# A separate tile for the third pair of quarter sums in a two-layer decoder trunk

## The chip, the cores and the metric

The kernel runs on one NeuronCore of a Trainium2 chip. The metric is the device time of one execution in microseconds (us); lower is better. Where a spread is given, it is that of three timed executions.

## The reference

A trunk of two layers over 256 tokens of width 2048, all in fp32. Layer 0 mixes tokens with forgetting attention (16 heads of 128), layer 1 with a mixture of three dilated windows (8 heads). Each mixer and each MLP stands behind an RMSNorm and adds into the residual stream:

```
def sq_relu_mlp(h, w_up, w_down):
    a = jax.nn.relu(h @ w_up)          # (256 x 2048) @ (2048 x 8192)
    return (a * a) @ w_down            # (256 x 8192) @ (8192 x 2048)

for i in range(DEPTH):                 # DEPTH = 2
    h = rms_norm(x, mix_norm_g[i])
    x = x + (fox_attention if i % 2 == 0 else dilated_attention)(h, ...)
    h = rms_norm(x, mlp_norm_g[i])
    x = x + sq_relu_mlp(h, mlp_w_up[i], mlp_w_down[i])
```

The change concerns the two MLPs, above all their product with `w_up`.

## The kernel before

**Tiles and engines.** Every weight matrix is read once from HBM, in tiles of 256 rows by 512 columns (512 KB, here called a *raw*: two row blocks of 128 x 512). TensorE (PE) multiplies in fp32r, so each raw is split into a high part and a low part: ScalarE (ACT) copies the raw into `wh` (L403), VectorE (DVE) subtracts that from the raw into `wl` (L404). A product is three matmuls, high x high, high x low, low x high, of 512 columns each (L452 to L454 for a plain raw, L1108 to L1110 for what follows).

**Units.** The raws are loaded in the order of a list `plan`, and split and multiplied in the order of a list `units`. There are `W_BUFS` = 5 pairs of `wh` and `wl`: when PE has used a unit, `split` prepares the unit five places later. There are `RAW_BUFS` = 5 raw buffers. After each split `next_load` marks in `spent` the raws that are no longer needed, moves the counter `done` forward over them, *in the order of the plan*, and issues loads until five raws beyond `done` are under way. All those loads (L378) stand in one queue, SyncE's (SP), which issues in order and waits at each load until the buffer it writes is free. The same queue carries the round trips through memory that transpose the activations: four writes `held` and one read `back` for each tile (L359).

**Wide halves.** Five of the 16 column groups of each `w_up` (list `WIDE`) are computed in pairs of column groups by seven products of half-size blocks in place of eight (the Strassen-Winograd scheme). For each pair of row blocks `pr` = 0 to 7, two raws are loaded crosswise: X1 holds the quarters B11 and B22, X2 holds B12 and B21. From them come three pairs of half-size operands, each a unit of its own and each with two products (`PRODUCTS`), so six matmuls:

- *crossed*: DVE first makes the differences X2 - B22 in a tile `quarters` with the tag `sd` (L400). Then X2 itself is split. Then DVE makes the third pair, one sum and one difference of quarters, **in place in X2** (L406, L407).
- *differences*: the tile `quarters` is split.
- *sums*: the third pair is split, read from X2's buffer.

A fourth kind (`what` = 3) is one plain product for each row pair. These units are woven in between plain raws of the other products, so that the order of units round a slot is: crossed, differences, a plain raw R0, sums, one or two more plain raws, the next crossed. In the plan the order is X1, X2, R0, R1, (R2), next X1, next X2. `add_slot` and `wide_slots` lay this down when the program is written; nothing is decided at run time.

**What the raw buffers do round a slot.** After the split of *crossed* X1 is spent and X2 is not, so `done` stops at X2: one load is issued there. After *differences* and R0 none is. After *sums* X2 and R0 are spent together, and two loads are issued.

**Token sums.** The other operand of those products are sums of blocks of the normalized activations. `token_sums` makes them for each `pr`, in a tile `room`, and splits them into a high and a low tile. These 16 tiles have to live through the whole MLP and lie in buffers that the attention layers use: the list `SUM_TAGS` names them, `vh` and `vl` (the attention values' two parts) for `pr` = 6, `pT` and `t1` for `pr` = 7. The tag `s` with five buffers holds the scores and is idle during the MLP but for the tables of the second mixer.

**After a wide half** `wide_chain` combines the six PSUM banks, squares, and hands over to `turn_up`, which transposes the result by the round trip `turned`, `held`, `back` and splits it into `aTh` and `aTl` (L1051, L1055, L1058), the operands of the product with `w_down`.

Of the kernel before, what the change touches and what calls it, by code (L numbers as in the profile page):

```python
# [9 lines left out]
F32 = mybir.dt.float32  # L10
F32R = mybir.dt.float32r
# [6 lines left out]
P = 128  # L18
# [3 lines left out]
NC = 512  # L22
NX = D // NC
KC = D // P
# [13 lines left out]
RAW_SUB = 2  # L38
PARTS = ((0, 12), (12, 16))
OUT_PARTS = ((0, 12), (12, 14), (14, 16))  # L40
S_BUFS = 5
# [2 lines left out]


PRODUCTS = (((0, 1, 5), (1, 0, 0)), ((2, 0, 1), (3, 1, 3)), ((4, 0, 2), (5, 1, 6)))
SUM_TAGS = ("kh3", "kl3", "kh4", "kl4", "kh5", "kl5", "q0", "q1", "q2", "qkw0", "qkw1", "qkw2", "vh", "vl", "pT", "t1")

WIDE = ((1, 0), (2, 0), (2, 2), (3, 0), (3, 2))
WIDE_FROM = 15  # L50
# [74 lines left out]
def trunk(ctx: ExitStack, tc, x, fox_w_in, fox_b_f, fox_q_gain, fox_k_gain, fox_w_out, dil_w_in,  # L125
          dil_q_gain, dil_k_gain, dil_w_out, mix_norm_g, mlp_norm_g, mlp_w_up, mlp_w_down, out):
    nc = tc.nc
# [5 lines left out]
    def clear(steps):  # L133

        return steps + (jobs.now + steps + 1 + shift[0]) % 2
# [21 lines left out]
    work = ctx.enter_context(tc.tile_pool(name="work", bufs=1))  # L157
# [210 lines left out]
    raws, splits = [], []  # L368

    def load():  # L370
        i = state["raw"]
        if i >= len(plan):
            return
        t = wpool.tile([P, RAW_SUB, NC], F32, tag="raw", name=f"raw{i}", bufs=RAW_BUFS)
        for (k, columns), src in plan[i]:
            hold(t)
            for rows in [slice(x, x + 1) for x in range(RAW_SUB)] if i == 1 else [None]:
                nc.sync.dma_start(t[:, k if rows is None else rows, columns], src if rows is None else src[:, rows])  # L378
        raws.append(t)
        state["raw"] += 1  # L380

    def split(parts=(slice(0, W_SUB),)):
        i = state["split"]
        if i >= len(units):
            return
        hi = wpool.tile([P, W_SUB, NC], F32R, tag="wh", name=f"wh{i}", bufs=W_BUFS)
        lo = wpool.tile([P, W_SUB, NC], F32R, tag="wl", name=f"wl{i}", bufs=W_BUFS)
        splits.append((hi, lo))
        state["split"] += 1
        for part in parts:  # L390
            split_part(i, part)
        if parts:
            next_load()

    def split_part(i, part):
        n, of = units[i]
        raw, (hi, lo) = raws[n], splits[i]
        if of == "crossed":
            sums_of[0] = work.tile([P, RAW_SUB, NC], F32, tag="sd", name=f"quarters{n}", bufs=1)
            nc.vector.tensor_sub(sums_of[0], raw, raws[n - 1][:, 1, :].unsqueeze(1).to_broadcast([P, RAW_SUB, NC]))  # L400
        elif of == "differences":
            raw = sums_of[0]
        nc.scalar.copy(hi[:, part, :], raw[:, part, :])  # L403
        nc.vector.tensor_sub(lo[:, part, :], raw[:, part, :], hi[:, part, :].bitcast(F32))  # L404
        if of == "crossed":
            nc.vector.tensor_add(raw[:, 0, :], raw[:, 0, :], sums_of[0][:, 1, :])  # L406
            nc.vector.tensor_sub(raw[:, 1, :], raws[n - 1][:, 0, :], raw[:, 0, :])  # L407

    sums_of, spent = [None], set()

    def next_load():


        n, of = units[state["split"] - 1]
        spent.update({"rows": (n,), "crossed": (n - 1,), "sums": (n,)}.get(of, ()))
        while state["done"] in spent:
            state["done"] += 1
        while state["raw"] < min(len(plan), state["done"] + RAW_BUFS):
            load()
# [3 lines left out]
    def in_turn(w, apart=NC // 2):  # L423
        return w.rearrange("p (b h n) -> p b n h", n=apart, h=2)
# [135 lines left out]
    def token_sums(tag):  # L560


        to = work.tile([P, 4, P], F32, tag="vw", name=f"room_{tag}", bufs=1)
        for pr in range(KC // 2):
            yield (tag, pr)
            yield clear(4)
            whole = hT[tag][pr]
            nc.vector.tensor_add(to.rearrange("p (i t) n -> p i (t n)", i=2), whole[:, :, 0, :].bitcast(F32),
                                 whole[:, :, 1, :].bitcast(F32))
            a12, a22, a11, a21 = (to[:, i, :] for i in range(4))  # L570
            nc.vector.tensor_add(a21, a21, a22)
            nc.vector.tensor_sub(a11, a11, a21)
            nc.vector.tensor_add(to[:, 0:2, :], to[:, 0:2, :], a11.unsqueeze(1).to_broadcast([P, 2, P]))
            yield 2
            hi, lo = (work.tile([P, 4, P], F32R, tag=SUM_TAGS[2 * pr + x], name=f"sums_{tag}_{pr}_{x}", bufs=1)
                      for x in range(2))
            nc.scalar.copy(hi, to)
            yield 1
            nc.vector.tensor_sub(lo, to, hi.bitcast(F32))
            sumT[tag, pr] = hi, lo  # L580
            jobs.done.add(("sums", tag, pr))

    sumT = {}
# [171 lines left out]

    def values(name):
        whole = work.tile([P, NC], F32, tag="vw", name=f"{name}w", bufs=1)
        v_hi, v_lo = (work.tile([P, NC], F32R, tag=f"v{x}", name=f"{name}{x}", bufs=1) for x in "hl")
        return whole, v_hi, v_lo

    def scores(ps, t, q, k, i):

# [335 lines left out]
    def slot_steps(tag, banks, what, pr, then):  # L1098

        hi, lo = splits[used[0]]  # L1100
        for bank, i, a, of in [(0, i, 4, pr + i) for i in range(2)] if what == 3 else [(*x, pr) for x in PRODUCTS[what]]:
            wh, wl = (in_turn(w[:, i, :]) for w in (hi, lo))
            if a < 4:
                ah, al = (x[:, a, :] for x in sumT[tag, of])
            else:
                ah, al = (hT[tag][of][:, a % 2, x, (a - 4) // 2 * P:((a - 4) // 2 + 1) * P] for x in range(2))
            alone = {"skip_group_check": bank == 0}
            nc.tensor.matmul(banks[bank], ah, wh, start=what < 3 and of == 0, stop=False, **alone)  # L1108
            nc.tensor.matmul(banks[bank], ah, wl, start=False, stop=False, **alone)
            nc.tensor.matmul(banks[bank], al, wh, start=False, stop=of == KC // 2 - 1, **alone)  # L1110
        then()
        used[0] += 1
        split()
        shift[0] ^= 1
        jobs.tick()

    def mlp(tag, **after):
# [3 lines left out]
        def one(b, n, what, pr):  # L1121
            if pr == 0 and what in (0, 2):
                pools = ((ps_acc, f"acc{1 - turn['only']}"),) if what else ((ps_tp, "tp"), (ps_sc, "sc"))
                banks[2 * what:] = [pool.tile([P, NC], F32, tag=of, name=f"wide_{tag}_{b}_{n}_{of}{i}")
                                    for pool, of in pools for i in range(2)]
            if what < 3:
                jobs.need(("sums", tag, pr))

            def then():
                if what == 2 and pr == KC // 2 - 1:  # L1130
                    jobs.spawn(wide_chain(list(banks), tag, b, n, aTs[b]))
                if what == 3 and pr == KC // 2 - 2:
                    jobs.reach((f"{tag}a{b}", "crossed", n))

            slot_steps(tag, banks, what, pr, then)

        jobs.spawn(token_sums(tag))
        woven.update(count=0, do=one, due={})
        for at, slot in wide_slots():
# [58 lines left out]
    row_blocks = [slice(i, i + 1) for i in range(W_SUB)]  # L1198
    split(())
    split_part(0, row_blocks[0])  # L1200
    jobs.spawn(first(0))
    split_part(0, row_blocks[1])
    next_load()
    split(())
    split_part(1, row_blocks[0])
# [4 lines left out]
    def opening():  # L1210
        yield 1
        split_part(1, row_blocks[1])
        next_load()
        yield 2
        split(row_blocks)
        yield 1
        split()
        for _ in range(5):
            yield 2
            split()  # L1220
        yield 1
        del issued["opening"]
        while state["split"] - used[0] < W_BUFS:
            yield 4
            split()
# [7 lines left out]
    tag = "n0"  # L1233
    for j in range(4):
        qT, kT = zip(*(heads_pairs(f"f{j}_{i}", i) for i in range(2)))
        vt = values(f"fv{j}")
        product(keys_h(tag), lhs_h(tag), lambda acc: qk_chain(
            acc, tag, ("fq", j), [(0, 2, FOX_G, qT[0]), (2 * P, 2, FOX_G, qT[1])]))
        if j == 0:
            jobs.need("wf")  # L1240
            gate(tag)
        product(keys_h(tag), lhs_h(tag), lambda acc: qk_chain(
            acc, tag, ("fk", j), [(0, 2, FOX_G + 1, kT[0]), (2 * P, 2, FOX_G + 1, kT[1])]))

        for hh in range(4):
            jobs.spawn(fox_head(j, hh, qT, kT, vt))
        product(keys_h(tag), lhs_h(tag), lambda acc: v_chain(acc, tag, ("fv", j), vt))
# [42 lines left out]
```

## Time and profile before

| | |
|---|---|
| median of three runs | 2124.59 us (2123.57 to 2125.57) |
| the profiled execution's own time | 2127.25 us |
| its span, first to last instruction | 2125.5 us |
| PE busy | 2091.7 us (98%) |
| DVE busy | 1733.9 us (82%) |
| ACT busy | 1288.6 us (61%) |
| moved by DMA | 539.02 MB, mean 254 GB/s |
| wide halves of the first MLP | from 402.1 us to 928 us of the span |
| wide halves of the second MLP | from 1500.4 us to 2023 us of the span |

Busy time counts an engine as busy while at least one of its instructions is under way. Matmuls overlap, and a PE that is fed without a pause is busy all the time; a row of waits names the instruction that waited, then the one that ended the wait, and gives the total in us, the number of times, and the longest. PEld is TensorE's loading of the stationary operand, which waits a little before the matmul does.

### The profile page before, as it was taken

To read this page: it belongs to the slowest core of one execution; us is meant where nothing else is said; L and a number is where in the kernel's file an instruction comes from. 1 tells how busy PE (TensorE), PEld (TensorE's weight loads), DVE (VectorE), ACT (ScalarE), POOL (GpSimd) and SP (SyncE) were. 2 spreads that over 40 slices of the span, in tenths; PEclk is the share of its full clock that TensorE was granted. 3 is DMA by queue.
4 is the path that set the end of the run, shared out by engine and by line. 5 is a ranking of instruction groups with operands and counts; after the bars stand their busy time and mean duration, and the time that the engine had idled before them with its cause. 6 is when DMAs were issued, how large, how long until landed. Compare 5 with 4: busy or idle time off the path is not lost.

```text
span 2125.5 us, 28747 instructions
## 1 busy us (share of the span) xinstructions
PE 2091.7 (98%) x9835; PEld 1819.3 (86%) x9835; DVE 1733.9 (82%) x2213; ACT 1288.6 (61%) x1775; POOL 135.0 (6%) x142
## 2 busy tenths in 40 slices
PE   9999999989999999999999999999999999999999
PEld 7888888878888888888888888888787888888888
DVE  6888876998889889887768787767998899898874
ACT  6565654756566657574656565646666576666562
POOL 2000000000010011010001010000000100110100
PEclk9999999999999999999999999999999999999999
DMA  8889887778898898897977776868778888988895
GB/s 255 254 263 271 249 248 232 242 229 256 252 282 270 253 280 262 266 283 247 283 236 238 245 237 210 269 205 242 243 230 274 263 276 264 272 268 272 264 290 169
DMA packets 385875, 539.02 MB, mean 254 GB/s; under 512 B 43753, under 2 KB 177217, under 8 KB 385729
## 3 DMA queue, kind: packets, MB, share of 16 engines
q1 hardware_dynamic: 371488, 524.21, 78.4%
q0 software_dynamic: 13824, 12.59, 3.7%
q8 instruction: 77, 1.26, 0.2%
q14 instruction: 70, 0.57, 0.1%
q10 hardware_dynamic: 416, 0.39, 0.1%
HBM read 484.09 MB, written 40.39 MB: 247 GB/s over the span
## 4 chain that ended last, share of the span: by engine, by line
PE 53%; DVE 21%; DMA 15%; issue 5%; ACT 3%; SPq 2%; DVEq 0%; ACTq 0%
PE acc L454 15%; PE acc L452 15%; PE acc L453 15%; DVE wl L404 11%; DMA raw<-in_mlp_w_up_dram 10%; DVE quarters L400 3%; DMA raw<-in_mlp_w_down_dram 2%; ACT wh L403 2%; DVE raw L406 2%; SPq L359 1%; DMA back_n1a<-held_n1a 1%; DMA back_n3a<-held_n3a 1%; DMA held_n1a<-turned_n1a 1%; DVE turned_n3a L1026 1%; DVE turned_n1a L1026 1%
## 5 line engine op out<-in xcount | busy, mean ns | idle before, releaser
L403 ACT CAST wh<-raw 128x1024 fp32r<-128x1024 f32 (+1 forms) x843 | 867.1, 1044 | 652.8 <-PE acc L454 283.6
L404 DVE TENSOR_TENSOR wl<-raw,wh 128x1024 fp32r<-128x1024 f32 (+1 forms) x843 | 1007.0, 1213 | 276.3 <-ACT wh L403 267.2
L452 PE MATMUL acc<-wh,hT_n 128*128 128x512 f32 x1280 | 488.0, 381 | 0.0
L453 PE MATMUL acc<-wl,hT_n 128*128 128x512 f32 x1280 | 486.9, 380 | 0.3 <-DVE wl L404 0.3
L454 PE MATMUL acc<-wh,hT_n 128*128 128x512 f32 x1280 | 486.3, 380 | 0.0
L453 PEld LDWEIGHTS acc<-wl,hT_n 128*128 128x128 f32 x1280 | 242.9, 190 | 35.3 <-DVE wl L404 2.5
L454 PEld LDWEIGHTS acc<-wh,hT_n 128*128 128x128 f32 x1280 | 242.6, 190 | 34.7 <-DVE hT_n L600 0.4
L452 PEld LDWEIGHTS acc<-wh,hT_n 128*128 128x128 f32 x1280 | 242.8, 190 | 34.0 <-ACT a_n1a L1003 0.4
L454 PE MATMUL acc<-wh,aTl_n1a 128*128 128x512 f32 x512 | 195.5, 382 | 4.6 <-DVE aTl_n1a L1058 2.3
L452 PE MATMUL acc<-wh,aTh_n1a 128*128 128x512 f32 x512 | 195.3, 381 | 2.5 <-ACT y_n L963 2.5
L453 PE MATMUL acc<-wl,aTh_n1a 128*128 128x512 f32 x512 | 195.3, 381 | 0.0
L454 PE MATMUL acc<-wh,aTl_n3a 128*128 128x512 f32 x480 | 182.3, 380 | 2.8 <-DVE aTl_n3a L1058 2.3
L452 PE MATMUL acc<-wh,aTh_n3a 128*128 128x512 f32 x480 | 182.5, 380 | 0.8 <-ACT y_n L963 0.7
L453 PE MATMUL acc<-wl,aTh_n3a 128*128 128x512 f32 x480 | 182.2, 380 | 0.9 <-DVE wl L404 0.9
L400 DVE TENSOR_TENSOR quarters<-raw,raw 128x1024 f32<-128x1024 f32 x80 | 97.8, 1222 | 67.3 <-DMA raw<-in_mlp_w_up_dram 56.6
L964 POOL DMA_DIRECT2D x<-y_n x96 | 84.4, 1360 | 995.4 <-ACT y_n L963 789.1
L403 ACT CAST wh<-quarters 128x1024 fp32r<-128x1024 f32 x80 | 83.8, 1047 | 51.8 <-DVE quarters L400 49.9
L454 PEld LDWEIGHTS acc<-wh,aTl_n1a 128*128 128x128 f32 x512 | 97.3, 190 | 20.0 <-DVE aTl_n1a L1058 3.1
L452 PEld LDWEIGHTS acc<-wh,aTh_n1a 128*128 128x128 f32 x512 | 97.2, 190 | 17.5 <-ACT y_n L963 3.7
L453 PEld LDWEIGHTS acc<-wl,aTh_n1a 128*128 128x128 f32 x512 | 97.2, 190 | 14.6 <-DVE wl L404 0.8
L454 PEld LDWEIGHTS acc<-wh,aTl_n3a 128*128 128x128 f32 x480 | 90.7, 189 | 17.0 <-DVE aTl_n3a L1058 3.1
L452 PEld LDWEIGHTS acc<-wh,aTh_n3a 128*128 128x128 f32 x480 | 90.7, 189 | 15.4 <-ACT y_n L963 2.4
(673 smaller groups left out, 2902.8 us busy)
## 6 DMA issues: line engine op xcount, KB each, us to landing
raw<-in_mlp_w_up_dram SPq DMA_DIRECT2D x296, 512.0 KB, 4.8
raw<-in_mlp_w_down_dram SPq DMA_DIRECT2D x256, 512.0 KB, 5.7
raw<-in_dil_w_in_dram SPq DMA_DIRECT2D x192, 256.0 KB, 3.7
raw<-in_fox_w_in_dram SPq DMA_DIRECT2D x94, 512.0 KB, 4.8
raw<-in_fox_w_out_dram SPq DMA_DIRECT2D x32, 512.0 KB, 5.0
raw<-in_dil_w_in_dram SPq DMA_DIRECT2D x32, 512.0 KB, 5.9
raw<-in_dil_w_out_dram SPq DMA_DIRECT2D x32, 512.0 KB, 4.4
x<-y_n POOLq DMA_DIRECT2D x96, 128.0 KB, 7.3
```

Source lines behind the costliest of these rows:

```text
L359: nc.sync.dma_start(dst, src)
L400: nc.vector.tensor_sub(sums_of[0], raw, raws[n - 1][:, 1, :].unsqueeze(1).to_broadcast([P, RAW_SUB, NC]))
L403: nc.scalar.copy(hi[:, part, :], raw[:, part, :])
L404: nc.vector.tensor_sub(lo[:, part, :], raw[:, part, :], hi[:, part, :].bitcast(F32))
L406: nc.vector.tensor_add(raw[:, 0, :], raw[:, 0, :], sums_of[0][:, 1, :])
L452: nc.tensor.matmul(acc[t], ah[:, tok], hi, start=first, stop=False)
L453: nc.tensor.matmul(acc[t], ah[:, tok], lo, start=False, stop=False)
L454: nc.tensor.matmul(acc[t], al[:, tok], hi, start=False, stop=last)
L964: nc.gpsimd.dma_start(xt[n][:, t, h * HC:h * HC + HC], y, accum_op=ALU.add)
L1026: nc.vector.transpose(tiles[t].rearrange("p (j b r) -> p b j r", j=4, b=4), rows[t].rearrange("p (b j c) -> p b j c", j=4, c=32))
```

## The change

1. The third pair of quarters no longer overwrites X2. It is written into a tile of its own with the tag `v`, one buffer of 128 x 2 x 512, made in *crossed* beside the tile `sd`; *sums* is split from it.
2. `next_load` therefore counts both X1 and X2 as spent after *crossed*, and none after *sums*.
3. The tag `v` is what `vh` and `vl` were: the attention values' two parts become one tile with two halves.
4. The token sums of `pr` = 6 take `pT` and `t1`. Those of `pr` = 7 go into three tiles of the tag `s`, each 128 x 3 x 128: three of the four blocks' high parts in the first, their low parts in the second, the fourth block's two parts in the third. Their split takes two copies and two subtractions in place of one each.

```
-SUM_TAGS = (..., "qkw2", "vh", "vl", "pT", "t1")
+SUM_TAGS = (..., "qkw2", "pT", "t1")
...
         if of == "crossed":
-            sums_of[0] = work.tile([P, RAW_SUB, NC], F32, tag="sd", name=f"quarters{n}", bufs=1)
-            nc.vector.tensor_sub(sums_of[0], raw, raws[n - 1][:, 1, :].unsqueeze(1).to_broadcast([P, RAW_SUB, NC]))
-        elif of == "differences":
-            raw = sums_of[0]
+            quarters[:] = [work.tile([P, RAW_SUB, NC], F32, tag=x, name=f"{x}_{n}", bufs=1) for x in ("sd", "v")]
+            nc.vector.tensor_sub(quarters[0], raw, raws[n - 1][:, 1, :].unsqueeze(1).to_broadcast([P, RAW_SUB, NC]))
+        elif of != "rows":
+            raw = quarters[("differences", "sums").index(of)]
         nc.scalar.copy(hi[:, part, :], raw[:, part, :])
         nc.vector.tensor_sub(lo[:, part, :], raw[:, part, :], hi[:, part, :].bitcast(F32))
         if of == "crossed":
-            nc.vector.tensor_add(raw[:, 0, :], raw[:, 0, :], sums_of[0][:, 1, :])
-            nc.vector.tensor_sub(raw[:, 1, :], raws[n - 1][:, 0, :], raw[:, 0, :])
+            nc.vector.tensor_add(quarters[1][:, 0, :], raw[:, 0, :], quarters[0][:, 1, :])
+            nc.vector.tensor_sub(quarters[1][:, 1, :], raws[n - 1][:, 0, :], quarters[1][:, 0, :])
...
-        spent.update({"rows": (n,), "crossed": (n - 1,), "sums": (n,)}.get(of, ()))
+        spent.update({"rows": (n,), "crossed": (n - 1, n)}.get(of, ()))
...
+            if pr < KC // 2 - 1:
+                split_sums = [[work.tile([P, 4, P], F32R, tag=SUM_TAGS[2 * pr + x], ...) for x in range(2)]]
+            else:
+                three = [work.tile([P, 3, P], F32R, tag="s", name=f"sums_{tag}_{pr}_{x}", bufs=S_BUFS) for x in range(3)]
+                split_sums = [three[0:2], (three[2][:, 0:1, :], three[2][:, 1:2, :])]
...
     def values(name):
         whole = work.tile([P, NC], F32, tag="vw", name=f"{name}w", bufs=1)
-        v_hi, v_lo = (work.tile([P, NC], F32R, tag=f"v{x}", name=f"{name}{x}", bufs=1) for x in "hl")
-        return whole, v_hi, v_lo
+        both = work.tile([P, 2, NC], F32R, tag="v", name=f"{name}hl", bufs=1)
+        return whole, both[:, 0], both[:, 1]
```

More of the change, by code (lines that the diff above doesn't have):

```diff
@@ L46 @@
 PRODUCTS = (((0, 1, 5), (1, 0, 0)), ((2, 0, 1), (3, 1, 3)), ((4, 0, 2), (5, 1, 6)))
-SUM_TAGS = ("kh3", "kl3", "kh4", "kl4", "kh5", "kl5", "q0", "q1", "q2", "qkw0", "qkw1", "qkw2", "vh", "vl", "pT", "t1")
+SUM_TAGS = ("kh3", "kl3", "kh4", "kl4", "kh5", "kl5", "q0", "q1", "q2", "qkw0", "qkw1", "qkw2", "pT", "t1")
 WIDE = ((1, 0), (2, 0), (2, 2), (3, 0), (3, 2))
@@ L405, in split_part @@
         if of == "crossed":
-            nc.vector.tensor_add(raw[:, 0, :], raw[:, 0, :], sums_of[0][:, 1, :])
-            nc.vector.tensor_sub(raw[:, 1, :], raws[n - 1][:, 0, :], raw[:, 0, :])
-    sums_of, spent = [None], set()
+            nc.vector.tensor_add(quarters[1][:, 0, :], raw[:, 0, :], quarters[0][:, 1, :])
+            nc.vector.tensor_sub(quarters[1][:, 1, :], raws[n - 1][:, 0, :], quarters[1][:, 0, :])
+    quarters, spent = [], set()
     def next_load():
         n, of = units[state["split"] - 1]
-        spent.update({"rows": (n,), "crossed": (n - 1,), "sums": (n,)}.get(of, ()))
+        spent.update({"rows": (n,), "crossed": (n - 1, n)}.get(of, ()))
         while state["done"] in spent:
@@ L574, in token_sums @@
             yield 2
-            hi, lo = (work.tile([P, 4, P], F32R, tag=SUM_TAGS[2 * pr + x], name=f"sums_{tag}_{pr}_{x}", bufs=1)
-                      for x in range(2))
-            nc.scalar.copy(hi, to)
+            if pr < KC // 2 - 1:
+                split_sums = [[work.tile([P, 4, P], F32R, tag=SUM_TAGS[2 * pr + x], name=f"sums_{tag}_{pr}_{x}", bufs=1)
+                               for x in range(2)]]
+            else:
+                three = [work.tile([P, 3, P], F32R, tag="s", name=f"sums_{tag}_{pr}_{x}", bufs=S_BUFS) for x in range(3)]
+                split_sums = [three[0:2], (three[2][:, 0:1, :], three[2][:, 1:2, :])]
+            sumT[tag, pr] = tuple([x[:, i, :] for x, _ in parts for i in range(x.shape[1])] for parts in
+                                  (split_sums, [pieces[::-1] for pieces in split_sums]))
+            at = 0
+            spans = []
+            for hi, lo in split_sums:
+                spans.append(to[:, at:at + hi.shape[1], :])
+                nc.scalar.copy(hi, spans[-1])
+                at += hi.shape[1]
             yield 1
-            nc.vector.tensor_sub(lo, to, hi.bitcast(F32))
-            sumT[tag, pr] = hi, lo
+            for (hi, lo), of in zip(split_sums, spans):
+                nc.vector.tensor_sub(lo, of, hi.bitcast(F32))
             jobs.done.add(("sums", tag, pr))
@@ L1103, in slot_steps @@
             if a < 4:
-                ah, al = (x[:, a, :] for x in sumT[tag, of])
+                ah, al = (x[a] for x in sumT[tag, of])
             else:
```

## The prediction

> **What bounds the kernel now.** I read the page first, then the waits of TensorE's weight loads (PEld), then the waits of VectorE (DVE), each for the whole span and for the stretches of the wide halves.
>
> ```profile
> span 2125.5 us, 28747 instructions
> PE 2091.7 (98%) x9835; PEld 1819.3 (86%) x9835; DVE 1733.9 (82%) x2213; ACT 1288.6 (61%) x1775; POOL 135.0 (6%) x142
> ```
>
> PE is busy for 98% of the span, and the change removes no matmul. All it can give back is idle time, 2125.5 - 2091.7 = 33.8 us. The largest item of that idle time is this, as the weight loads see it, and behind it stands a wait of DVE's:
>
> ```profile
> PEld wide_n_sc L1109 <- DVE wl L404: 19.6, 17, 3.7
> DVE quarters L400 <- DMA raw<-in_mlp_w_up_dram: 56.6, 36, 2.9
> ```
>
> The bank `wide_n_sc` belongs to the unit *differences*. Seventeen times PE stood there because the low part of the differences wasn't ready; and 36 times DVE, before it could even begin a slot (L400), stood idle for a raw. A slot's chain on DVE is long: L400, the low part of crossed, L406, L407, the low part of differences. When the raw is late, that last step is late. The same wait by stretches, in this order: 400 to 470, 470 to 500, 500 to 940, 1490 to 1565, 1565 to 1600, 1600 to 2030 us:
>
> ```profile
> PEld wide_n_sc L1109 <- DVE wl L404: 6.7, 3, 3.3
> PEld wide_n_sc L1109 <- DVE wl L404: 0.5, 1, 0.5
> PEld wide_n_sc L1109 <- DVE wl L404: 3.1, 4, 1.3
> PEld wide_n_sc L1109 <- DVE wl L404: 6.1, 3, 3.7
> PEld wide_n_sc L1109 <- DVE wl L404: 0.4, 2, 0.2
> PEld wide_n_sc L1109 <- DVE wl L404: 2.8, 4, 1.4
> ```
>
> Nearly two thirds lie in the first wide half of each MLP. That stage differs from the others:
>
> ```profile
> 426.00:463.00 37.00, 31.62 (x136) 25.96 (x134) 34.06 (x44) 19.64 (x26) 0.00 (x0) 0.95 0.70 223
> 1526.00:1561.00 35.00, 30.14 (x129) 24.36 (x127) 32.53 (x43) 19.88 (x26) 0.00 (x0) 0.95 0.71 232
> 570.00:640.00 70.00, 70.00 (x326) 61.31 (x325) 63.44 (x66) 47.66 (x60) 7.04 (x8) 1.00 0.89 277
> 740.00:830.00 90.00, 86.64 (x398) 74.33 (x397) 77.91 (x78) 58.68 (x72) 10.57 (x12) 1.00 0.90 275
> ```
>
> The columns are the stretch's length, busy PE, PEld, DVE, ACT, POOL, then granted clock, DMA share and GB/s. In the first two rows DVE is busy for 34.06 of 37 us and 32.53 of 35 us, because the token sums are made there too: DVE sets the pace, and DMA runs at 0.70. In the last two DVE has more room and DMA is at 0.90.
>
> **Why the raw is late.** One slot, seen on SP's queue and on DVE:
>
> ```profile
> 773.85 2.64 SPq L378 DMA_DIRECT2D raw<-in_mlp_w_up_dram  x2
> 773.13 0.69 DVE L407 TENSOR_TENSOR raw<-raw,raw 128x512 f32<-128x512 f32 x1
> 773.74 1.22 DVE L404 TENSOR_TENSOR wl<-quarters,wh 128x1024 fp32r<-128x1024 f32 x1
> 774.88 2.36 DVE L404 TENSOR_TENSOR wl<-raw,wh 128x1024 fp32r<-128x1024 f32 x2
> 782.68 1.22 DVE L400 TENSOR_TENSOR quarters<-raw,raw 128x1024 f32<-128x1024 f32 x1 [2.88 <-DMA raw<-in_mlp_w_up_dram]
> ```
>
> The first load (next X1) goes out at 773.85, when L407 ends. The second (next X2) goes out about 2.64 - 0.37 = 2.3 us later (an issue takes some 0.4 us), behind the low part of R0: it stands in the queue at the split of *sums*, where X2 is released in the program before. The X2 that it brings is what DVE waits 2.88 us for.
>
> **The change, part by part.** *The loads.* With the third pair in a tile of its own, both loads stand at *crossed* and wait for L407 alone; the next one waits for R0's low part instead of that of *sums*. In the slot shown X2 is issued at some 774.2 instead of 776.1, 1.9 us earlier. Where the queue carried a round trip in between, more is won. Next come three such places in the first wide halves, one by SP and DVE:
>
> ```profile
> 420.13 0.39 SPq L378 DMA_DIRECT2D raw<-in_mlp_w_up_dram  x1
> 425.88 0.98 SPq L378 DMA_DIRECT2D raw<-in_mlp_w_up_dram  x2
> 446.23 4.95 SPq L378 DMA_DIRECT2D raw<-in_mlp_w_up_dram  x2
> 1517.70 0.39 SPq L378 DMA_DIRECT2D raw<-in_mlp_w_up_dram  x1
> 1524.38 0.98 SPq L378 DMA_DIRECT2D raw<-in_mlp_w_up_dram  x2
> 426.25 2.35 DVE L404 TENSOR_TENSOR wl<-raw,wh 128x1024 fp32r<-128x1024 f32 x2
> 429.98 1.23 DVE L400 TENSOR_TENSOR quarters<-raw,raw 128x1024 f32<-128x1024 f32 x1 [1.37 <-DMA raw<-in_mlp_w_up_dram]
> ```
>
> X2 would go out some 5.3, 4.2 and 6.3 us earlier there (the difference less one issue). Where three plain raws lie between two slots this holds; where two lie between, X2's load stands at the earlier *crossed* already and only a plain raw comes sooner. DVE's idle time for raws is, from 400 to 470, 1490 to 1565, 500 to 940 and 1600 to 2030 us:
>
> ```profile
> DVE quarters L400 <- DMA raw<-in_mlp_w_up_dram: 2.4, 2, 1.4
> DVE quarters L400 <- DMA raw<-in_mlp_w_up_dram: 1.9, 1, 1.9
> DVE quarters L400 <- DMA raw<-in_mlp_w_up_dram: 22.6, 13, 2.9
> DVE quarters L400 <- DMA raw<-in_mlp_w_up_dram: 24.6, 16, 2.8
> ```
>
> *First wide halves.* DVE works without a pause here but for these waits, so PE gets back only what DVE gets back: 2.4 us and 1.9 us. The lead of 4.2 us and more covers waits of at most 1.9 us, so I take all of it, and the rest of the 6.7 and 6.1 us stays, as DVE's own work. The small waits from 470 to 500 (0.5) and 1565 to 1600 (0.4 in two) follow waits for a raw and go: 0.4 + 0.1, by the rate of the next paragraph. Together 2.4 + 0.4 + 1.9 + 0.1 = 4.8 us.
>
> *The other wide halves.* What an idle weight load costs PE:
>
> ```profile
> 864.22 0.38 PE L1108 MATMUL wide_n_sc<-wh,sums_n 128*128 128x512 f32 x1
> 865.20 0.19 PEld L1109 LDWEIGHTS wide_n_sc<-wl,sums_n 128*128 128x128 f32 x1 [1.01 <-DVE wl L404]
> 865.52 0.38 PE L1110 MATMUL wide_n_sc<-wh,sums_n 128*128 128x512 f32 x1
> ```
>
> Fed without a pause a matmul takes 70.00 / 326 = 0.215 us (the stretch 570 to 640). Here two took 865.52 - 864.22 = 1.30 us, 0.87 too much for an idle of 1.01: 0.14 less than the row says. The eight waits (3.1 in 4, 2.8 in 4, longest 1.4) cost 5.9 - 8 x 0.14 = 4.8 us. The longest is 1.4 us and the least lead some 1.9 us, so all eight go, even though DVE's waits of up to 2.9 us shrink to about 1 and don't vanish: the five units prepared ahead cover that. One of them (810 us) stands at a slot whose own X2 isn't earlier; it goes only because DVE comes out of the slot before it sooner. The bounds of this part are 0 and 4.8.
>
> *DVE's arithmetic.* L400, L406 and L407 keep their sizes; only the output of the last two moves. Nothing waits for the tile `v`: the previous *sums* was split earlier on the same engine. Cost 0. If that order failed, DVE would wait for one low part, 1.22 us (the L404 row above), 80 times; the program's order excludes it.
>
> *Token sums of the last pair.* One subtraction more and one copy more for each MLP. The operation that is cut in two:
>
> ```profile
> 413.29 0.68 DVE L579 TENSOR_TENSOR sums_n<-room_n,sums_n 128x512 fp32r<-128x512 f32 x1
> ```
>
> The two parts do the same work; the second adds between nothing and a whole 0.68 us, 1.4 us for both MLPs if nothing hid it, and less by far since it is a quarter of the size. I take 0 and leave the rest to the range; the cover is DVE's slack after the fifth slot. *Tags.* `t1` is taken one pair sooner, long after the squares of the norm that use it were issued; the `s` tiles are freed before the second mixer's tables need them; the values' two parts are written one behind the other and read together. I count these at 0. If a tag were still held, ACT's copy of the sums would wait, and behind it all high parts.
>
> **The sum.** 4.8 + 4.8 = 9.6 us. The profiled execution took 2127.25 us, 1.75 more than its span; it would take 2117.65. It lies 2.66 above the median of the three runs, so for the median I forecast 2124.59 - 9.6 = 2115.0 us, with a range of its own of 2112 to 2119.
>
> **The rivals.** *DMA is full, and X2 lands no sooner.* In the later halves DMA's share is 0.89 to 0.90, so loads issued sooner may only queue longer. Then the eight waits there stay, and the first halves, at 0.70, still give 4.8: 2119.8 us. Against it: between 773.85 and 776.1 SP had issued one raw and held the next back. By the row's share a tenth of DMA's time is free. [...]
>
> *Round trips come late: slower.* The reads `back` and the writes `held` that stand between *crossed* and *sums* now stand behind two more loads in SP's queue and in the DMA engines. ACT runs in order, so a cast L1051 that waits for `back` holds up every high part behind it, and with them PE.
>
> ```profile
> DMA to landing us min/median/max: 3.7/5.7/8.6
> L1051 ACT CAST aTh_n1a<-back_n1a x26: 610/614/624, 431.0 to 925.7; 128x512 fp32r<-128x512 f32 x26
> L1051 ACT CAST aTh_n3a<-back_n3a x26: 610/614/619, 1529.8 to 2020.7; 128x512 fp32r<-128x512 f32 x26
>   DMA back_n1a<-held_n1a: 0.6, 1
> ```
>
> The first line is for the reads `back`, the last is ACT's idle time for them within the first MLP's wide halves. The program allows six steps of six matmuls, 36 x 0.215 = 7.7 us, from the read to the cast; the median landing leaves 2.0 us. Two raws more ahead are 1.05 MB, at 275 GB/s 3.8 us. So a pair could be 1.8 us late; with 26 pairs in the two MLPs and about 1 us of it reaching PE behind the units prepared ahead, that is 26 us, less the 9.6: 2141 us. It decides from 0.4 us a pair. Against it: only 0.6 us of such waits today, the bytes are the same, and those moves stood behind loads that waited for the same DVE work already.
>
> *The clock too: faster still.*
>
> ```profile
> 434.80:438.20 3.40, 0.88 (x4) 0.80 (x5) 3.37 (x6) 2.64 (x4) 0.00 (x0) 1.00 0.65 204
> 438.20:441.60 3.40, 3.40 (x10) 2.50 (x9) 3.40 (x4) 1.86 (x3) 0.00 (x0) 0.50 0.43 100
> ```
>
> After a stretch in which PE was busy for 0.88 of 3.4 us the granted clock was 0.50 for 3.4 us. The mean clock of 0.95 over 37 and 35 us in the two first halves (above) says that it happened once in each, and cost 1.85 and 1.75 us. With those waits shortened by 1.4 and 1.9 us the halving may not come: some 3.4 us more, 2111.6. I don't count it, since DVE sets the pace there, and what PE gains it waits out at the next slot. [...]
>
> *The change does not do what it says.* If the buffer that X2's load takes is one freed only at *sums*, nothing moves: 2124.6 us. For it: the second load goes out at the end of R0's low part, not that of *sums*, so the buffers aren't handed out in the plan's order. Against it: at *crossed* two are free at once.
>
> **How the numbers follow.** Forecast 0.52, full DMA 0.14, late round trips 0.12, clock 0.11, no move 0.11. A measurement here can tell 0.2%, 4.2 us: faster means below 2120.3. The forecast and the clock are faster, full DMA lies at the edge and I give it 0.08 and 0.06: faster 0.71, same 0.17, slower 0.12. The range runs from the clock case with 2 us of spare, 2109.5, to no move, 2124.6, and leaves out the slow case.
>
> **What would show it.** Two loads L378 at the end of each L407; SP's wait for `sums` gone. DVE's 56.6 us for raws at L400 down to a third or less. PEld's 19.6 us at `wide_n_sc` down to about 8, all of it in the first halves. Wrong if ACT waits for `back` by several us, if the eight later waits are still there, or if PE's idle time falls at L1109 and grows elsewhere.

## The result, and the profile after

| | before | after |
|---|---|---|
| median | 2124.69 us (2123.57 to 2125.57, four runs) | 2096.99 us (2096.43 to 2100.19, four runs) |
| ratio | | 0.9873 (95% interval 0.9856 to 0.9890) |
| the profiled execution and its span | 2127.25, 2125.5 us | 2096.45, 2094.6 us |

The change takes 27.7 us off, nearly three times the 9.6 us of the forecast, and the time lies below the range. The sign was right, the size was not. The chances were set on "faster" by 0.71.

These lines of the page answer to those of before: the span, the busy times, and the chain of work that ended last, by engine.

```profile
span 2094.6 us, 28771 instructions
PE 2080.3 (99%) x9835; PEld 1825.0 (87%) x9835; DVE 1730.1 (83%) x2215; ACT 1294.0 (62%) x1777; POOL 134.8 (6%) x142
PE 87%; DVE 6%; DMA 3%; issue 1%; ACT 1%; SPq 1%; POOL 0%; DVEq 0%; ACTq 0%; POOLq 0%
```

Before, the last of these read:

```profile
PE 53%; DVE 21%; DMA 15%; issue 5%; ACT 3%; SPq 2%; DVEq 0%; ACTq 0%
```

The chain that sets the end used to run through PE for half of its length, and through DVE and the DMA for over a third. Now it is PE for 87%. Two things in the first two lines deserve a look. PE's *busy* time fell by 11.4 us although it does the same 9835 matmuls. And the span of the profiled execution fell by 2125.5 - 2094.6 = 30.9 us, nearly all of the 33.8 us that the prediction held to be the most there was.

The slot that the prediction showed looks like this now (the timeline of the changed kernel, a slot of the same wide half; columns are start, duration, engine, line):

```profile
767.64 1.22 DVE L400 TENSOR_TENSOR sd<-raw,raw 128x1024 f32<-128x1024 f32 x1
769.91 0.69 DVE L406 TENSOR_TENSOR v<-raw,sd 128x512 f32<-128x512 f32 x1
770.63 0.69 DVE L407 TENSOR_TENSOR v<-raw,v 128x512 f32<-128x512 f32 x1
770.66 1.06 SPq L378 DMA_DIRECT2D raw<-in_mlp_w_up_dram  x2
```

Two loads go out nearly together: the first at 770.66, when L406 ends, the second some 0.7 us later, when L407 ends. L400 has no wait before it. The waits of the whole span, in the order of the prediction's list (the weight loads, then DVE, then SP's queue for the first and for the second of these loads):

```profile
PEld wide_n_sc L1120 <- DVE wl L404: 9.7, 5, 2.9
DVE sd L400 <- DMA raw<-in_mlp_w_up_dram: 8.1, 13, 2.5
SPq L378 <- DVE v L406: 142.9, 68, 3.1
SPq L378 <- DVE v L407: 17.6, 67, 1.6
```

Before they were 19.6 us in 17, 56.6 us in 36, and this:

```profile
SPq L378 <- DVE raw L407: 271.7, 70, 6.2
```

That row is the wait of the one load that stood at *crossed* then, so it answers to the 142.9 us of L406; the 17.6 us are all that the second load waits beyond it.

**Where the other 20 us came from.** The quickest reading is to count matmuls in stretches of equal length. Before, then after, from 402 to 470, 470 to 940, 1490 to 1565 and 1565 to 2030 us; the second column is PE's busy time with the number of matmuls:

```profile
402.00:470.00 68.00, 60.21 (x266) 50.40 (x265) 63.56 (x82) 39.04 (x50) 0.00 (x0) 0.97 0.70 217
470.00:940.00 470.00, 462.83 (x2125) 401.27 (x2124) 407.87 (x416) 301.66 (x365) 40.50 (x47) 1.00 0.87 267
1490.00:1565.00 75.00, 69.98 (x311) 58.85 (x310) 71.55 (x100) 47.69 (x68) 1.07 (x1) 0.98 0.73 224
1565.00:2030.00 465.00, 459.15 (x2115) 398.05 (x2114) 404.51 (x413) 297.54 (x359) 38.41 (x44) 1.00 0.87 268
```
```profile
402.00:470.00 68.00, 63.85 (x286) 54.51 (x285) 67.28 (x88) 43.72 (x57) 0.00 (x0) 0.97 0.76 239
470.00:940.00 470.00, 468.91 (x2171) 410.92 (x2170) 413.62 (x424) 311.51 (x376) 42.95 (x50) 1.00 0.88 273
1490.00:1565.00 75.00, 71.66 (x323) 61.66 (x322) 74.24 (x91) 48.27 (x62) 0.00 (x0) 0.98 0.79 247
1565.00:2030.00 465.00, 465.00 (x2156) 408.14 (x2155) 406.15 (x417) 305.98 (x368) 41.80 (x48) 1.00 0.89 274
```

Each MLP has five wide halves, and each takes a pair of column groups, so it is ten of the 16 groups that are computed this way. In the first and third stretch, mostly the first wide halves, the changed kernel does 20 and 12 matmuls more, at 0.216 us (470.00 / 2171) some 6.9 us; the forecast gave these stages 4.8. In the second and fourth it does 46 and 41 more, 18.8 us; the forecast gave them 4.8. So the surprise lies in the later halves, where PE already looked nearly full.

What PE waited for there stood in the same list of waits of before's weight loads, below the one row that the prediction quoted:

```profile
PEld acc L452 <- ACT y_n L963: 6.1, 9, 2.2
PEld acc L453 <- DVE wl L404: 5.1, 11, 1.1
PEld acc L454 <- DVE aTl_n3a L1058: 3.1, 2, 2.4
PEld acc L454 <- DVE aTl_n1a L1058: 3.1, 2, 2.4
PEld acc L454 <- DVE aTl_n1a L1055: 3.1, 2, 1.7
PEld acc L454 <- DVE aTl_n3a L1055: 1.2, 2, 0.9
```

The second row is the low part of a plain raw; it fell to 1.6 us. The other five, 16.6 us together, are waits in the product with `w_down`: for a PSUM bank that ACT hasn't emptied yet (`y_n`), and for the low part of an activation that DVE hasn't made yet (`aTl`). None of these five names a raw. After, no wait for `y_n` is left and two for `aTl` of 0.2 us each. I also summed the extra spacing of successive matmuls over their usual pitch, from the trace's start times, by the place in the program. In the slots it went from 19.5 to 10.3 us, in the product with `w_down` from 16.6 to 0.2, in stretches of halved clock from 6.2 to 2.9, and in the rest from 13.0 to 11.3. The gains are 9.2, 16.4, 3.3 and 1.7 us, together 30.6 of the 30.9.

### The profile page after: what moved, and what is told of

Read it like the earlier page. It is cut to its first block, busy times and chain, and to the rows that moved or that the text cites. A ratio compares the mean times of both kernels' runs of the same rounds, so it can differ in the third digit from the quotient of the medians.

```text
span 2094.6 us, 28771 instructions
## 1 busy us (share of the span) xinstructions
PE 2080.3 (99%) x9835; PEld 1825.0 (87%) x9835; DVE 1730.1 (83%) x2215; ACT 1294.0 (62%) x1777; POOL 134.8 (6%) x142
## 4 chain that ended last, share of the span: by engine, by line
PE 87%; DVE 6%; DMA 3%; issue 1%; ACT 1%; SPq 1%; POOL 0%; DVEq 0%; ACTq 0%; POOLq 0%
PE acc L452 23%; PE acc L453 23%; PE acc L454 23%; DVE wl L404 3%; PE wide_n_tp L1120 2%; PE wide_n_tp L1119 2%; PE wide_n_tp L1121 2%; DMA raw<-in_mlp_w_up_dram 2%; PE wide_n_sc L1120 2%; PE wide_n_sc L1121 2%; PE wide_n_sc L1119 1%; PE wide_n_acc L1121 1%; PE wide_n_acc L1119 1%; PE wide_n_acc L1120 1%; ACT wh L403 1%
## 5 line engine op out<-in xcount | busy, mean ns | idle before, releaser
L404 DVE TENSOR_TENSOR wl<-raw,wh 128x1024 fp32r<-128x1024 f32 (+1 forms) x763 | 919.8, 1214 | 305.8 <-ACT wh L403 292.1
L403 ACT CAST wh<-raw 128x1024 fp32r<-128x1024 f32 (+1 forms) x763 | 787.7, 1045 | 531.0 <-PE acc L454 350.3
L403 ACT CAST wh<-sd 128x1024 fp32r<-128x1024 f32 x80 | 84.0, 1050 | 85.8 <-DVE sd L400 64.4
L403 ACT CAST wh<-v 128x1024 fp32r<-128x1024 f32 x80 | 84.0, 1050 | 50.6 <-PE acc L454 38.9
L400 DVE TENSOR_TENSOR sd<-raw,raw 128x1024 f32<-128x1024 f32 x80 | 97.6, 1220 | 8.3 <-DMA raw<-in_mlp_w_up_dram 8.1
```

The costliest lines, as they stand in the source:

```text
L400: nc.vector.tensor_sub(quarters[0], raw, raws[n - 1][:, 1, :].unsqueeze(1).to_broadcast([P, RAW_SUB, NC]))
```

## The experiments

All ratios are against the kernel before, timed beside each run. Where a run is set against the changed kernel in us, that is the difference of two medians that were not timed beside each other; by the ratios these differences come out up to some 2 us otherwise.

**1. The tags alone.** The changed kernel, its tags and token sums, but with the third pair in place and the marks as before.

```
-  quarters[:] = [work.tile(..., tag=x, ...) for x in ("sd", "v")]
+  quarters[:] = [work.tile(..., tag="sd", ...), raw]
...
-  spent.update({"rows": (n,), "crossed": (n - 1, n)}.get(of, ()))
+  spent.update({"rows": (n,), "crossed": (n - 1,), "sums": (n,)}.get(of, ()))
```

> The tags of the changed kernel (token sums of the last two pairs moved, the values' parts in one tile), but the third pair of quarter sums still made in place in X2, and X2 marked spent at sums. Theory A (the gain comes from the raws issued sooner): nothing changes against the kernel before, 2124.7 us, within 3. Theory C (a part of the gain that the prediction has not got comes from the moved tiles): up to 18 us of the 27.7 appear here, some 2107.

Measured: 2124.19 us, ratio 0.9991 (0.9979 to 1.0004). The moved tags and token sums give nothing that can be told from no change.

**2. The tile of its own, the mark left late.** Only the second edit above: X2's buffer is free early, but its successor's load stays at *sums* in the queue.

> The changed kernel, but X2 is marked spent at sums as before: its buffer is free at L406, while the loads stand later in SP's queue, behind R0's split and the round trips between. Theory A1 (what counts is that the buffer is free, since SP runs ahead in its queue): nearly all of the gain, 2097 to 2103 us. Theory A2 (what counts is the load's place in the queue): nearly none, 2118 to 2125.

Measured: 2105.01 us, ratio 0.9912 (0.9897 to 0.9927). By the ratios that is 0.0088 x 2126.4 = 18.7 us (2126.4 is the kernel before, timed beside it), and the whole change is 0.0127 x 2124.7 = 27.0 us; by the intervals each is known to 3 or 4 us. The result lies between the two theories. Some 18.7 come with the tile alone, whose buffer is free at L406 in place of the split of *sums*, and the other 8.3 with the load's place in the queue. The tile could also have helped because L406 no longer overwrites what the split of X2 still reads, but no trace shows a wait to be saved there: in the kernel before too, DVE had no idle time ahead of L406 or L407.

**3 and 4. Only some of the slots.** The tile and the early mark for the three row pairs behind which two plain raws lie (`pr` 2, 5, 7), then for the five behind which three lie.

```
-            quarters[:] = [... for x in ("sd", "v")]
+            quarters[:] = [... for x in ("sd", "v")[:1 + apart[n]]]
+            quarters[1:] = quarters[1:] or [raw]       # apart[n]: pr in (2, 5, 7), or in (0, 1, 3, 4, 6)
...
-  "crossed": (n - 1, n)}
+  "crossed": (n - 1, n) if apart.get(n) else (n - 1,), "sums": (n,)}
```

> The separate tile only for row pairs 2, 5 and 7, which two plain raws follow before the next slot (after 7 the wide half's products end); for the others X2 is overwritten as before. By the prediction's step only plain raws are issued sooner there, X2's load is not. Theory A (X2's lead alone): within 4 us of the kernel before, 2121 to 2125. Theory B (any raw issued sooner feeds the whole queue's lead): about three eighths of the gain, some 2114.

> The separate tile only for row pairs 0, 1, 3, 4 and 6, which three plain raws follow before the next slot. Theory A: nearly the whole gain, 2097 to 2101 us. Theory B: about five eighths, some 2107.

Measured: 2110.21 us, ratio 0.9932 (0.9917 to 0.9947), and 2100.56 us, ratio 0.9890 (0.9873 to 0.9906). The first speaks against theory A, the second came out at theory A's time and not at B's, so neither had it right. The first is the telling one: at these slots the prediction saw only "a plain raw" come sooner and gave them nothing of their own; they alone give 0.0068 x 2126.4 = 14.5 us. The two gains, 14.5 and 23.4 (0.0110), add up to 38 us where both together give 27. So the gain can't be priced slot by slot: each set of slots does part of the other's work.

**5. One raw buffer fewer in the changed kernel** (`RAW_BUFS` 4 for 5).

> The changed kernel with four raw buffers in place of five. Theory B (every raw's lead over PE is what all the waits share; from the issue of a plain raw's load to PE's use of it 12.9 us before and 14.6 after the change, on the mean over the wide halves): one raw less in flight takes about 2.5 us of that lead, below the kernel before: slower than it, 2125 to 2160 us, with the waits back both at the slots and at the products with w_down. Theory A (it is X2 in its own buffer): the slots keep their gain, at most 2115.

Measured: 2168.78 us, ratio 1.0200 (1.0181 to 1.0220), slower than the range expected. Not all of that lies in the MLPs: ACT's waits for raws of the second mixer's weights grew from 12.6 to 25.8 us. The waits for `y_n` and `aTl` return with it:

```profile
PEld acc L454 <- DVE aTl_n1a L1066: 5.8, 3, 3.0
PEld acc L452 <- ACT y_n L974: 5.7, 6, 2.5
```

With less lead for every raw, the product with `w_down` waits again for things that no load writes.

**6. The token sums' additions on GpSimd** (L568 to L573 of the changed kernel as `nc.gpsimd`), to free DVE in the first wide halves.

> The changed kernel with the four additions of each pair's token sums on GpSimd in place of VectorE (1.7 us of VectorE's time for each of 16 pairs). If VectorE's work sets the pace of the first wide half of each MLP, as the prediction said, the 8.7 us of waits left there and the 2.9 us of halved clock go for the greater part: 2087 to 2092 us. Rival: GpSimd makes them so late, or holds VectorE up so far, that the slots wait for the sums: 2097 or slower.

Measured: 2115.91 us, ratio 0.9951 (0.9933 to 0.9969), 19 us slower than the changed kernel. That is the rival of the expectation, and it leaves the question of DVE's pace to run 9: GpSimd is too slow at it, and PE now waits for `a_n1a` and `a_n3a`, 3.9 us each, the relus that stand behind the copies of the sums on ACT. Columns are shortest, median and longest in ns.

```profile
L568 POOL TENSOR_TENSOR room_n<-hT_n x16: 1268/2124/6802, 363.6 to 1547.9; 128x512 f32<-128x512 f32 x16
```

**7. Half the bytes of X1 and X2, in the kernel before.** Half of the columns are loaded and each is used twice; the instructions on DVE and ACT keep their sizes.

```
-  plan.append([((slice(0, RAW_SUB), slice(0, NC)), crosswise)])
+  plan.append([((slice(0, RAW_SUB), slice(0, NC // 2)), crosswise[:, :, 0:NC // 2])])
```

> The kernel before, but of X1 and X2 only half the columns are loaded, and used twice, so that the operands are not the reference's; all instructions of the engines keep their sizes, and the third pair stays in place. X1 and X2 land sooner, by some 1 us, and all buffers are freed as before. Theory B: both the waits at the slots (19.5 us) and those at the products with w_down (16.6 us) shrink; 2105 to 2115 us. If it is the tile of its own and not the raws' lateness: 2122 to 2126.

Measured: 2104.87 us, ratio 0.9898 (0.9878 to 0.9919). Raws that land sooner (the halves took 3.0 us from issue to landing in the median, where all raws of `w_up` took 4.8 before) give 20 us without the new tile. No wait for `y_n` is left and the waits for `aTl` fall from 10.5 to 4.6 us.

**8. The round trips on another queue.** In the kernel before, `held` and `back` are issued by GpSimd in the two MLPs, so that they don't stand between loads in SP's queue.

> The kernel before with the round trips of the two MLPs (writes and reads of the transposes) issued from GpSimd's queue in place of SP's, so that they and the raws' loads no longer stand behind each other. Theory Q (the 16.6 us of waits at the products with w_down come from round trips stuck behind loads in SP's queue): those go, the slots' stay, some 2108 to 2112 us. Theory B (they come from ACT and VectorE, which wait in order for raws): those stay, 2120 us or more, and slower still if GpSimd issues its many small writes more slowly.

Measured: 2143.85 us, ratio 1.0072 (1.0050 to 1.0094); its six times spread from 2132.65 to 2146.09, and the trace is of the fastest. The waits for `aTl` grow from 10.5 to 14.8 us:

```profile
PEld acc L454 <- DVE aTl_n1a L1058: 5.5, 3, 2.5
PEld acc L454 <- DVE aTl_n3a L1055: 3.5, 2, 2.8
ACT aTh_n3a L1051 <- DMA back_n3a<-held_n3a: 20.9, 8, 8.1
```

This run does not decide between the two theories, since it made the round trips themselves later: ACT's waits for `back`, of which the last row is one half, grew from 11.7 to 40.3 us. What speaks against theory Q is the kernel before. Within the wide halves of its first MLP ACT waited for `back` only 0.6 us (the prediction shows the row), and ahead of two late `aTl` at 509 and 512 us it stood for a raw and then made both `aTh` without a wait for `back`:

```profile
503.30 1.05 ACT L403 CAST wh<-raw 128x1024 fp32r<-128x1024 f32 x1 [3.93 <-DMA raw<-in_mlp_w_down_dram]
506.10 1.14 ACT L1051 CAST aTh_n1a<-back_n1a 128x512 fp32r<-128x512 f32 x2
```

**9. Three additions left out.**

```
-            nc.vector.tensor_add(a21, a21, a22)
-            nc.vector.tensor_sub(a11, a11, a21)
-            nc.vector.tensor_add(to[:, 0:2, :], to[:, 0:2, :], a11...)
```

> The changed kernel without the three small additions of the token sums (L571 to L573, together about 1.0 us of VectorE for each of the eight pairs of a wide half, 16 us in the kernel); it leaves out the combining of the token sums, so these keep their plain parts. Theory D (what is left in the first halves is VectorE's pace: it is busy 69.28 of 70 us there): TensorE's waits for wl, 9.7 us, fall to under 4 us, the halved clocks at 445 and 1527 go, and the time is 5 to 9 us under the changed kernel's, 2088 to 2092 us. Rival R (the slots there are short because the raws or the order of the queue hold them, and VectorE is merely in step): the waits stay within 2 us of 9.7 and the time is 2096 to 2098 us.

Measured: 2085.41 us, ratio 0.9810 (0.9793 to 0.9827), 11.6 us under the changed kernel, somewhat more than the 5 to 9 us of theory D. The wait at `wide_n_sc` falls from 9.7 to 0.8 us and PE is fed without a pause where the changed kernel did 286 and 323 matmuls:

```profile
PEld wide_n_sc L1116 <- DVE wl L404: 0.8, 2, 0.5
402.00:470.00 68.00, 67.90 (x314) 58.88 (x313) 66.88 (x77) 46.02 (x58) 0.00 (x0) 1.00 0.83 264
1490.00:1565.00 75.00, 75.00 (x349) 65.52 (x348) 73.25 (x81) 49.09 (x59) 0.00 (x0) 1.00 0.84 272
```

So what was left in the first halves is DVE's pace. 16 us of its work were worth 11.6 us, and the clock is 1.00 in both stretches: both halvings that the changed kernel still had are gone.

**10. Half the bytes of X1 and X2 in the changed kernel** (the edit of 7).

> The changed kernel, with only half the columns of X1 and X2 loaded and each used twice, so these operands are not the reference's. Theory B (the early loads had already taken nearly all of the lateness of the raws away; what is left is VectorE's pace in the first halves): VectorE's waits for raws fall from 8.1 us to under 3 us and the time is 2093 to 2097 us, a gain of at most 4 us where the same halving gave the kernel before 20 us. Rival (raws still come late through ScalarE, which waits 87 us for them): another 8 us or more, 2089 us or less.

Measured: 2098.12 us, ratio 0.9871 (0.9854 to 0.9889). What gave the kernel before 20 us gives the changed kernel nothing, although ACT's waits for the raws of the two MLPs fell once more, from 87 to 40 us. So X1 and X2 no longer set the time by landing late.

**11 and 12. Can the DVE work be spread?** The wide halves begin one slot later (`WIDE_FROM` 18 for 15), so that more token sums are made before the first slot; then the same with the sums two steps sooner (`clear(2)` for `clear(4)`).

> The changed kernel with the wide halves begun one slot later (WIDE_FROM 18 for 15): the same work on every engine, but one pair of token sums more is made before the first slot, so about 2.4 us of VectorE's work (the rows L568 to L573 and L591) leaves the stretch in which it is busy 69.28 of 70 us, in each of the two MLPs. Theory D (VectorE's pace there is what is left): the waits for wl in the first halves fall from 9.7 us to about 5 us, and the time is 2 to 5 us under the changed kernel's 2097, 2092 to 2095 us. Rival R (the place of the slots doesn't matter, or what is won comes back where the last wide half now ends one slot later): 2096 us or more.

> As the run with the halves begun later, and the token sums of each pair also begin two steps sooner (clear(2) for clear(4)). Theory D: still more of the sums lies before the dense stretch, 2089 to 2094 us, under the run with the halves begun later alone. Rival: VectorE is busy 11.38 of 12 us just before the first slot too, so the sums made sooner only move the waits there, and the time is within 1.5 us of that run's.

Measured: 2112.60 us, ratio 0.9943 (0.9930 to 0.9956), and 2113.71 us, ratio 0.9946 (0.9932 to 0.9960). Both beat the kernel before and lose 16 us against the changed one. The first row is the wait that the theory was about, and it falls to 5.0 us as expected; the others show what it cost at other places:

```profile
PEld wide_n_sc L1120 <- DVE wl L404: 5.0, 5, 2.2
PEld acc L452 <- ACT aTh_n3a L1062: 7.0, 2, 6.0
PEld acc L452 <- ACT aTh_n1a L1062: 5.1, 2, 4.6
PEld acc L452 <- ACT a_n3a L1014: 4.3, 1, 4.3
955.00:965.00 10.00, 5.83 (x18) 4.04 (x17) 7.12 (x12) 3.86 (x6) 0.00 (x0) 0.79 0.99 311
2050.00:2060.00 10.00, 8.32 (x27) 6.35 (x28) 3.81 (x5) 3.59 (x6) 0.00 (x0) 0.67 0.46 173
```

The last wide half of each MLP ends a slot later, its round trip is not back when the product with `w_down` needs it (`aTh`), and the clock falls as well (0.79 and 0.67 in those ten us). That is rival R of the first of these runs, and more than it said; the second run came out within 1.1 us of the first, as its rival had it. The changed kernel is the fastest of those tried that compute everything.

## Why the prediction was right or wrong

**Right: the mechanism at a slot.** Two loads go out at *crossed*, one at the end of L406 and one at the end of L407 (the prediction had both at L407), and the second waits only 17.6 us in all. DVE's waits for raws at L400 fell from 56.6 to 8.1 us (forecast: to a third or less), and the eight later waits at `wide_n_sc` but for one of 1.3 us are gone. Its 19.6 us fell to 9.7 (forecast: about 8), all but that one in the first halves, 4.4 and 4.0. The slots as a whole gave 9.2 us of matmul spacing against the forecast 9.6.

**Right: nothing paid for it.** Arithmetic, tags and token sums at 0 are borne out by run 1. ACT's wait for `back` in the first MLP stayed as it was, 6.1 us before and 6.0 after, so the slower rival fell. Full DMA fell too: a load's median time from issue to landing stayed at 4.9 us, so loads issued sooner did land sooner, and from 470 to 940 us the core moved 273 GB/s in place of 267. With the loads moved, the rival of no change at all fell as well.

**Right, though first halves gained more than it said: DVE's pace there.** Run 9 shows it directly.

**Wrong: "the largest item of that idle time is this", and the sum that went on from it.** The prediction took the largest row of the weight loads' list and costed what the loads do to *that* wait. The five rows for `y_n` and `aTl`, 16.6 us together, it put at nothing without a reason; they don't name a raw. This is the step that failed: by the spacing of the matmuls that term measured 16.4 us, more than the whole forecast of 9.6. These waits do hang on the raws, by way of the engines' order. This is ACT, and then PE, in the kernel before:

```profile
735.42 1.06 ACT L403 CAST wh<-raw 128x1024 fp32r<-128x1024 f32 x1 [2.32 <-DMA raw<-in_mlp_w_up_dram]
739.90 1.06 ACT L403 CAST wh<-raw 128x1024 fp32r<-128x1024 f32 x1 [1.01 <-DMA raw<-in_mlp_w_down_dram]
744.17 1.56 ACT L963 ACTIVATE y_n<-acc,rstd_n 128x256 f32<-128x256 f32 x4
745.05 0.48 PE L452 MATMUL acc<-wh,aTh_n1a 128*128 128x512 f32 x1 [1.78 <-ACT y_n L963]
```

ACT stood 3.3 us for two raws, and then worked without a pause through what had queued up, the emptying of a bank among it; the profile books PE's 1.78 us to `y_n`. The prediction had the rows to see it: DVE's and ACT's waits for raws are waits of everything queued behind them, here 3.3 us of ACT's ahead of PE's 1.78 us. Runs 5 and 7 bear this out: less lead brings the waits back, and fewer bytes take those for `y_n` and over half of those for `aTl` away in the old kernel.

**Wrong: the lead was priced slot by slot.** "Where two lie between, X2's load stands at the earlier crossed already and only a plain raw comes sooner" was given no worth. Run 3 says 14.5 us. A load waits for the split of the raw that lay in its buffer (before, 662.6 us of SP's queue for `wl` in 469 waits over the whole span), and that split waits for its own raw (ACT's rows below): if one comes sooner, the next is issued sooner too, until the splits wait for PE and no longer for the DMA. ACT's waits before its casts show that turn, before and then after:

```profile
ACT wh L403 <- PE acc L454: 285.6, 205, 2.5
ACT wh L403 <- DMA raw<-in_mlp_w_up_dram: 194.1, 91, 4.6
ACT wh L403 <- DMA raw<-in_mlp_w_down_dram: 73.0, 64, 3.9
```
```profile
ACT wh L403 <- PE acc L454: 409.0, 299, 2.1
ACT wh L403 <- DMA raw<-in_mlp_w_up_dram: 55.7, 47, 3.9
ACT wh L403 <- DMA raw<-in_mlp_w_down_dram: 31.7, 20, 2.8
```

267 us of waiting for raws became 87, and 286 us of waiting for PE became 409. By the trace's times, a plain raw's load was issued on the mean 14.6 us ahead of PE's first use, and 12.9 before. That the loop closes in this way is argued from these rows and from runs 3 and 4; no run follows a single advance from slot to slot.

**Wrong: 33.8 us as a limit, and the clock.** PE's busy time is not a floor: the profile books a matmul of 0.38 us with 0.48 us behind a wait (at 512.36 us of the kernel before) and with 0.63 us at a granted clock of 0.50 (at 513.35 us), and the busy time fell by 11.4 us. In run 9 the whole span, 2082.6 us, is shorter than PE's busy time of before, 2091.7 us, with the same 9835 matmuls. PE's busy share is no measure here of what is left: for the same matmuls its busy time fell, while that of the weight loads did not (1819.3 and 1825.0 us). The clock rival was right that the clock would add something, 3.3 us, and wrong about which halvings would go. It named those of the first halves, and they stayed (a granted clock of 0.53 from 445.0 to 448.4 and from 1527.0 to 1530.4 us). Of the four before, from 438.2, 513.3, 977.5 and 1537.3 us on, the two that went (513.3 and 977.5) lay behind waits for `aTl` that the prediction hadn't costed.

## What to carry to other kernels

Before pricing an earlier load, list every wait of the engine that sets the time, not the largest one, and ask of each what its releaser had been doing just before: an engine that stands for a transfer can make its later products late, under other names (here ACT's 3.3 us for two raws, and then PE's 1.78 us for `y_n`). Where a load waits for the use of an earlier load, a lead is not spent at the place where it is won; look at whether the consumer waits for the transfer or for the producer downstream, and expect the gain to run until that turns. An experiment that shortens the transfer itself, before the change and after it, shows how much of the time hangs on it: here 20 us, then nothing that can be told from noise.

## What the runs showed of the hardware

In the kernel before, three matmuls that waited, and two stretches from 509.7 to 516.7 us round the second of them (the last three columns are the granted clock, the DMA share and GB/s):

```profile
509.43 0.48 PE L454 MATMUL acc<-wh,aTl_n1a 128*128 128x512 f32 x1 [0.95 <-DVE aTl_n1a L1055]
512.36 0.48 PE L454 MATMUL acc<-wh,aTl_n1a 128*128 128x512 f32 x1 [2.02 <-DVE aTl_n1a L1058]
975.81 0.48 PE L454 MATMUL acc<-wh,aTl_n1a 128*128 128x512 f32 x1 [1.34 <-DVE aTl_n1a L1055]
```
```profile
509.70:513.30 3.60, 1.58 (x7) 1.07 (x7) 3.60 (x6) 0.91 (x2) 0.00 (x0) 1.00 0.82 260
513.30:516.70 3.40, 3.40 (x9) 2.66 (x9) 1.66 (x3) 3.34 (x6) 0.00 (x0) 0.50 0.65 186
```

PE was idle for 0.95 and then for 2.02 us, and from 513.3 to 516.7 us the granted clock was 0.50. It was 0.50 from 977.5 to 980.9 us too, behind the 1.34 us of the third row and 0.29 us more of idle time. In the prediction's example PE was idle for 2.52 of the 3.4 us ahead. Yet the clock stayed at 1.00 from 745.05 to 748.45 us, behind a wait of 1.78 us, and from 1609.85 to 1613.25 us, behind another of 2.02 us, where PE had been idle for 2.51 of 3.45 us. What tells these waits apart the rows do not show.

An addition of 128 x 512 (L568) that takes 0.68 to 0.69 us on DVE in the changed kernel took 1.27 to 6.80 us on GpSimd by the profile, whose durations on that engine are rough (run 6). DVE's subtraction L404, 1.22 us in the median, took up to 2.30 us in that run, and at most 1.25 us in the changed kernel.
